# Weight parts that start 0 to 60 bytes past a multiple of 64, in a decoder trunk on one core

## The chip, the cores and the metric

The kernel runs on one core of a Trainium2 chip. The core has five engines that run side by side and meet at semaphores: TensorE (PE) multiplies, VectorE (DVE), ScalarE (ACT) and GpSimd (POOL) work element by element, and SyncE (SP) starts transfers. All but the transfers read and write the on-chip memory SBUF (128 partitions, each addressed in bytes) and the accumulators in PSUM. A matrix product on PE is a pair of instructions: LDWEIGHTS (in the profile "PEld") puts a 128x128 block, the weights, into the array, and MATMUL (in the profile "PE") streams the other operand, the moving one, through it. The metric is device time in microseconds (us) of one execution, lower is better; a kernel's time is the median of its runs.

## The reference

Two layers, each with three sub-layers around a residual stream of 512 tokens by 1024 features, in float32:

```python
h = modulate(x, norm_ffn1, sh1, sc1)
x = x + 0.5 * (1 + g1) * swiglu(h, ffn1_w1, ffn1_w3, ffn1_w2)        # 1024 -> 2816 -> 1024
h = modulate(x, norm_mix, sh2, sc2)
y = token_mix(h, ...)      # w_in; gated delta net and latent attention, 8 heads each; two branches; w_out
x = x + (1 + g2) * y
h = modulate(x, norm_ffn2, sh3, sc3)
x = x + 0.5 * (1 + g3) * swiglu(h, ffn2_w1, ffn2_w3, ffn2_w2)

def modulate(x, gain, shift, scale):
    return rms_norm(x, gain) * (1.0 + scale) + shift
def swiglu(h, w1, w3, w2):
    return (silu(h @ w1) * (h @ w3)) @ w2
```

The shifts, scales and gates come from a product of the conditioning vector with `ada_w`. Nearly all of the arithmetic is products of the 512-token activations with weight matrices that are read from main memory once.

## The kernel before

**Layout.** Features lie on the partitions, tokens along them: an activation is tiles of 128x512. A weight matrix is read in slabs of 128x1024 (eight blocks of 128x128), each 512 KB and used once.

**Two parts of each operand.** To keep float32 accuracy at one pass per product, each operand is split in a high part, rounded to the format fp32r, and a low part, the rest. A product is then three matmuls into one accumulator: high weights by high activations, high weights by low activations, low weights by high activations (`mm3`, line 130). In the profile the weight parts are called `whi` and `wlo`; the activation parts are `hhi` and `hlo`, or slices of the tiles `A`, `O`, `c3` and `L`.

**Where weight parts are made.** Three places make them: `slab` (line 116, most of the program: ACT copies `raw` to `whi`, line 124, and DVE subtracts, line 125), `parts` inside `weights` (line 604: the same for a whole slab at lines 606 and 607, where the feed-forward layers use sums of weight blocks and 256 tokens at a time), and `begin` (line 1473, the first product of layer 0). `whi` and `wlo` each have three buffers that are used in turn; a fourth kind of slab, given a `place`, lies in tiles `O` or `A` instead.

**How they are used.** `proj` (line 146) and `product` (line 621) make them the weights: the block that LDWEIGHTS loads is 128 columns, 512 bytes of each partition, of a slab. The moving operand is then an activation part of 512 or of 256 columns. In `mla_make` (line 1159) the sides change: the activation is the weights, and a `whi` or `wlo` of 384 or 512 columns is the moving operand.

**Order.** A tile framework places the instructions on the engines in an order of its own, except where the program asks to keep the written order; waits follow from which buffers an instruction reads and writes.

**Addresses.** The function `t` takes a buffer by its tag and the table `ALIGN`, line 72, gives the multiple at which buffers of a tag start; where it says nothing a buffer starts at a multiple of 32. In the built program the three `whi` start at bytes 141056, 145152 and 149248 of each partition and the three `wlo` at 153600, 157696 and 161792, all multiples of 256. Every other tile that is read as weights in blocks of 128 columns starts at a multiple of 64, except `identr` (186784, 32 past a multiple of 64), which is loaded 16 times. The two buffers `raw` start 32 past a multiple of 64, and the convolution (lines 750 to 759) has DVE read and write its tile `cv` at 4, 8 and 12 bytes past one.

Of the kernel before, what the change touches and what calls it, by code (L numbers as in the profile page):

```python
# [9 lines left out]
F32R = mybir.dt.float32r  # L10
# [5 lines left out]
P = 128  # L16
# [52 lines left out]
}  # L69


ALIGN = {"hhi": 2048, "hlo": 2048, "A": 2048, "kph": 256, "c3": 256, "L": 512, "O": 256, "whi": 256, "wlo": 256}


class Trunk:
    def __init__(self, ctx, tc, aps):
        self.tc = tc
        self.nc = tc.nc
        self.ap = aps
        self.sb = ctx.enter_context(tc.tile_pool(name="sb", bufs=1))  # L80
        self.ps = ctx.enter_context(tc.tile_pool(name="ps", bufs=1, space=bass.MemoryType.PSUM))
        self.count = 0
        self.pin = False
        self.ada_home = "L"
        self.units, self.body, self.ahead = [], None, None
        self.queue = []
        self.waiting = []
        self.quarters = {}
# [17 lines left out]
    def t(self, tag, shape, dt=F32):  # L106
        self.count += 1
        return self.sb.tile(list(shape), dt, tag=tag, name=f"{tag}_{self.count}", bufs=BUFS.get(tag, 1),
                            align_bytes=ALIGN.get(tag))

    def p(self, tag, shape=(P, SEQ)):
        self.count += 1
        return self.ps.tile(list(shape), F32, tag=tag, name=f"{tag}_{self.count}", bufs=BUFS[tag])


    def slab(self, src, n, place=None, home="raw", hold=False):

        nc = self.nc
        raw = self.t(home, [P, 1024])
        hi, lo = place or (self.t("whi", [P, 1024], F32R), self.t("wlo", [P, 1024], F32R))  # L120
        nc.sync.dma_start(raw[:, :n], src)
        for a in range(0, n, 512):
            s = slice(a, min(a + 512, n))
            both = [nc.scalar.copy(hi[:, s], raw[:, s]),  # L124
                    nc.vector.tensor_sub(lo[:, s], raw[:, s], hi[:, s].bitcast(F32))]  # L125
            for i in both if hold else ():
                self.order(i)
        return hi, lo
# [383 lines left out]
    def ffn(self, l, w, gate, finish, early, ahead=None):  # L512
# [88 lines left out]
        def weights(st):  # L601


            def parts(t):
                hi, lo = self.t("whi", [P, 1024], F32R), self.t("wlo", [P, 1024], F32R)
                nc.scalar.copy(hi, t)  # L606
                nc.vector.tensor_sub(lo, t, hi[:].bitcast(F32))  # L607
                return hi, lo

            yield parts(st["a11"])  # L610
            yield parts(st["f1"])
            f2, f4 = st["f1"], st["a12"]
            nc.vector.tensor_add(f2, f2, st["a11"])
            yield parts(f2)
            yield parts(f4)
            nc.vector.tensor_add(f4, f4, f2)
            yield parts(st["f3"])
            yield parts(f4)
            yield parts(st["a22"])
# [853 lines left out]
    def begin(self, ct, crow, vec, mod):  # L1473

        nc, ordered = self.nc, self.order
        self.pin = True

        ordered(nc.scalar.activation(self.t("sc4", [P, NT])[:, 0:1], self.one, AF.Silu))
        self.spin(2)
        wide = [self.p("sc") for _ in range(2)]  # L1480
        for (a, b), ps in zip(((0, SEQ), (SEQ, D)), wide):
            self.mm(ps, self.ones[0:1, :], crow[:, a:b], start=True, stop=True)

        sums = self.p("sm", [P, NT, P])
        for k in range(0, KT, 2):
            sq = [self.t("g", [P, SEQ]) for _ in range(2)]
            ordered(nc.scalar.activation(sq[0], self.x[:, k, :], AF.Square))
            if k == KT - 2:
                ordered(nc.vector.tensor_mul(sq[1], self.x[:, k + 1, :], self.x[:, k + 1, :]))
            else:  # L1490
                ordered(nc.scalar.activation(sq[1], self.x[:, k + 1, :], AF.Square))
            ordered(nc.vector.tensor_add(sq[0], sq[0], sq[1]))
            if k == 0:
                ss = sq[0]
                self.spin(2)
                continue
            if k == 2:
                ordered(nc.vector.tensor_add(sq[0], sq[0], ss))
            for i in range(NT):
                self.mm(sums[:, i, 0:1], sq[0][:, i * P:(i + 1) * P], self.one, start=k == 2 and i == 0,  # L1500
                        stop=k == KT - 2, skip_group_check=True)
        self.spin(1)
        ordered(nc.scalar.activation(self.cond, ct, AF.Silu))
        for i, ps in enumerate(wide):
            ordered(nc.scalar.activation(self.condb[:, i * SEQ:(i + 1) * SEQ], ps, AF.Silu))
        var, rn = (self.t("nv", [P, NT]) for _ in range(2))
        ordered(nc.vector.tensor_scalar(var, sums[:, :, 0], 1.0 / D, EPS, ALU.mult, ALU.add))
        nc.gpsimd.tensor_tensor(rn, var, self.power.to_broadcast([P, NT]), ALU.pow)
        shp = self.p("sm", [P, KT])
        self.hhi = self.t("hhi", [P, KT, SEQ], F32R)  # L1510
        self.hlo = self.t("hlo", [P, KT, SEQ], F32R)
        acts = self.hacts()
        gain = self.t("gain0", [P, KT])
        sc1 = self.t("sc1", [P, KT])
        ordered(nc.vector.tensor_scalar(sc1, vec[:, V_ADAB + KT:V_ADAB + 2 * KT], 1.0, None, ALU.add))
        n = BEGIN_SLABS
        prods, rb = [], None
        for k in range(KT):
            sc, sh = mod[:, KT + k:KT + k + 1], mod[:, k:k + 1]
            on_pe, on_pool = k in BEGIN_PE, k in BEGIN_POOL  # L1520
            self.ada_block(0, 1, k, mod)
            if not on_pe:
                self.ada_block(0, 0, k, mod)
            if k == 0:
                rp = self.p("po", [P, NT, P])
                for i in range(NT):
                    self.mm(rp[:, i, :], rn[:, i:i + 1].to_broadcast([P, P]), self.ident, start=True, stop=True)
                rb = rp[:].rearrange("p t c -> p (t c)")
            if k + 1 in BEGIN_PE:
                self.ada_block_pe(BEGIN_PE.index(k + 1), shp[:, k + 1:k + 2])  # L1530
            raw, hi = self.t("raw", [P, 1024])[:, :n * P], self.t("whi", [P, 1024], F32R)[:, :n * P]
            lo = self.t("wlo", [P, 1024], F32R)[:, :n * P]
            ordered(nc.vector.scalar_tensor_tensor(gain[:, k:k + 1], sc, sc1[:, k:k + 1],
                                                   vec[:, V_NORM + k:V_NORM + k + 1], ALU.add, ALU.mult))
            nc.sync.dma_start(raw, self.ap["w_begin"][k])
            h = self.t("g", [P, SEQ])
            ordered(nc.vector.scalar_tensor_tensor(h, self.x[:, k, :], gain[:, k:k + 1], rb, ALU.mult, ALU.mult))
            ordered(nc.vector.tensor_add(sh, shp[:, k:k + 1] if on_pe else sh, vec[:, V_ADAB + k:V_ADAB + k + 1]))
            ordered(nc.scalar.copy(hi, raw))
            xh, xl = acts[k]  # L1540
            ordered(nc.scalar.activation(xh, h, AF.Identity, bias=sh))
            ordered(nc.vector.tensor_sub(lo, raw, hi.bitcast(F32)))  # L1542
            if not on_pool:
                ordered(nc.vector.scalar_tensor_tensor(xl, h, sh, xh.bitcast(F32), ALU.add, ALU.subtract))
            for i, (a, b) in enumerate(HALVES):
                q = self.quarters.get((k // 2, i)) or self.quarter(k // 2, i, 4)
                ordered(nc.scalar.activation(q[:, k % 2, :], h[:, a:b], AF.Identity, bias=sh))
                if on_pool:
                    nc.gpsimd.tensor_sub(xl[:, a:b], q[:, k % 2, :], xh[:, a:b].bitcast(F32))  # L1549
            if k == 0:  # L1550
                prods = [self.p(tag) for tag in ("acc", "sc", "acc", "sc", "acc", "sm", "sm")]
            ws = [slice(m * P, (m + 1) * P) for m in range(n)]
            for w, p in zip(ws, prods):
                self.mm(p, hi[:, w], xh, start=k == 0, stop=False)
            for w, p in zip(ws, prods):
                self.mm(p, lo[:, w], xh, start=False, stop=False)
                self.mm(p, hi[:, w], xl, start=False, stop=k == KT - 1)
        ordered(nc.scalar.dma_start(self.ap["spill_c"], self.condb))
        self.pin = False
        return prods  # L1560
# [159 lines left out]
```

## Time and profile before

| what | value |
|---|---|
| median of 3 runs | 2707.18 us (2706.15 to 2711.35) |
| the profiled execution: its own time | 2707.17 us |
| its span, first to last instruction | 2705.4 us |
| PE busy, of the span | 2685.7 us, 99% |
| PEld busy | 2379.3 us, 88% |
| DVE busy | 1986.1 us, 73% |
| ACT busy | 1278.9 us, 47% |
| mean granted TensorE clock | 0.999 |
| matmuls, each with a weight load | 17042 |

"Busy" is the union of an engine's instructions in time. The duration of one matmul includes the time in which its results run out of the array, while the next has already begun: 389 ns for one of 512 columns, though the next starts 227 ns after it. So what a matmul costs in a stream is read from the distance between two starts, not from its duration; the same holds of weight loads. The chain of waits follows the work that ended last backwards, and lists in "pieces in order of time" how long it stayed on one engine, with the number of instructions.

### The profile page before, as it was taken

What the parts mean: (1) busy time and instruction counts of PE and PEld (TensorE: products, weight loads), DVE (VectorE), ACT (ScalarE), POOL (GpSimd) and SP (SyncE); (2) the same over time, 40 slices, a digit from 0 to 9 for tenths busy, and PEclk for the clock granted to TensorE, in tenths of its full rate; (3) what the DMA queues carried; (4) which work ended last, traced back from release to release, by engine and by line L of the source; (5) the groups of instructions that cost most, each with busy time, mean ns of one, the idle gap of its engine ahead of it and who ended that gap; (6) DMA issues with size and microseconds to landing.
All of it is one profiled execution on the core that took longest, in us unless ns stands there. A gap on an engine that the chain in (4) does not pass through costs nothing.

```text
span 2705.4 us, 44279 instructions
## 1 busy us (share of the span) xinstructions
PE 2685.7 (99%) x17042; PEld 2379.3 (88%) x17042; DVE 1986.1 (73%) x4113; ACT 1278.9 (47%) x2543; POOL 237.9 (9%) x375
## 2 busy tenths in 40 slices
PE   9999999999999999999999999999999999999999
PEld 7999997888888889998999999888888888998989
DVE  7887868776778777875677877786767687685745
ACT  4534454544457435443454444545434564453533
POOL 2100012000001011000010000120000111110000
PEclk9999999999999999999999999999999999999999
DMA  8778623212222554875528774232222225456642
GB/s 291 217 228 233 210 96 110 98 63 86 67 74 79 183 180 131 252 225 141 159 88 230 247 242 149 94 120 81 76 81 74 72 84 183 156 164 179 172 126 86
DMA packets 119108, 394.11 MB, mean 146 GB/s; under 512 B 13553, under 2 KB 16369, under 8 KB 118898
## 3 DMA queue, kind: packets, MB, share of 16 engines
q1 hardware_dynamic: 106370, 349.87, 38.8%
q0 software_dynamic: 10080, 36.70, 7.6%
q10 hardware_dynamic: 2448, 4.72, 0.5%
q8 instruction: 134, 2.20, 0.3%
q14 instruction: 76, 0.62, 0.1%
HBM read 376.03 MB, written 15.20 MB: 145 GB/s over the span
## 4 chain that ended last, share of the span: by engine, by line
PE 92%; DVE 4%; ACT 2%; DMA 1%; issue 1%; POOL 0%; SPq 0%; ACTq 0%; DVEq 0%; POOLq 0%
PE acc L96 65%; PE sc L96 17%; PE sm L96 6%; PE sm L101 2%; PE po L96 1%; ACT whi L124 1%; DMA raw<-in_w_out 0%; DVE wlo L125 0%; DVE L L283 0%; ACT g L1276 0%; DMA raw<-in_ffn_w 0%; PE po L101 0%; DVE wlo L1542 0%; DMA M<-in_x 0%; DVE mx L1271 0%
## 5 line engine op out<-in xcount | busy, mean ns | idle before, releaser
L124 ACT CAST whi<-raw 128x512 fp32r<-128x512 f32 (+2 forms) x548 | 315.7, 607 | 452.6 <-PE acc L96 231.1
L96 PE MATMUL acc<-hhi,whi 128*128 128x512 f32 (+1 forms) x1376 | 508.0, 369 | 0.0
L96 PE MATMUL acc<-hhi,wlo 128*128 128x512 f32 (+1 forms) x1376 | 489.4, 356 | 0.0
L96 PE MATMUL acc<-hlo,whi 128*128 128x512 f32 (+1 forms) x1376 | 488.8, 355 | 0.4 <-POOL hlo L1549 0.4
L125 DVE TENSOR_TENSOR wlo<-raw,whi 128x512 fp32r<-128x512 f32 (+2 forms) x548 | 374.8, 704 | 120.8 <-ACT whi L124 113.8
L96 PE MATMUL acc<-O,whi 128*128 128x512 f32 x1472 | 454.6, 390 | 0.0
L96 PE MATMUL acc<-A,whi 128*128 128x256 f32 (+1 forms) x1808 | 346.7, 291 | 1.1 <-ACT g L677 0.9
L96 PEld LDWEIGHTS acc<-O,whi 128*128 128x128 f32 x1472 | 274.9, 188 | 56.0
L96 PEld LDWEIGHTS acc<-hhi,wlo 128*128 128x128 f32 x1376 | 260.3, 189 | 38.5 <-DVE wlo L125 1.9
L96 PEld LDWEIGHTS acc<-A,whi 128*128 128x128 f32 x1808 | 286.0, 192 | 6.8 <-ACT g L677 1.3
L96 PE MATMUL acc<-O,wlo 128*128 128x512 f32 x736 | 286.8, 390 | 0.0
L96 PEld LDWEIGHTS acc<-hhi,whi 128*128 128x128 f32 x1376 | 261.1, 190 | 28.8 <-ACT whi L124 0.7
L96 PEld LDWEIGHTS acc<-hlo,whi 128*128 128x128 f32 x1376 | 261.2, 190 | 28.2 <-POOL hlo L1549 1.0
L96 PE MATMUL acc<-A,wlo 128*128 128x256 f32 (+1 forms) x904 | 262.6, 290 | 0.0
L606 ACT CAST whi<-L 128x1024 fp32r<-128x1024 f32 x140 | 147.2, 1052 | 201.7 <-issue 72.8
L607 DVE TENSOR_TENSOR wlo<-L,whi 128x1024 fp32r<-128x1024 f32 x140 | 171.2, 1223 | 35.9 <-ACT whi L606 35.1
L96 PEld LDWEIGHTS acc<-A,wlo 128*128 128x128 f32 x904 | 173.3, 192 | 2.5
L607 DVE TENSOR_TENSOR wlo<-raw,whi 128x1024 fp32r<-128x1024 f32 x105 | 128.5, 1224 | 60.8 <-ACT whi L606 59.8
L421 DVE SCALAR_TENSOR_TENSOR M<-acc,gate,M 128x512 f32<-128x512 f32 (+1 forms) x112 | 77.4, 691 | 128.7 <-PE acc L96 128.4
L606 ACT CAST whi<-raw 128x1024 fp32r<-128x1024 f32 x105 | 110.1, 1049 | 119.0 <-PE acc L96 47.2
L96 PEld LDWEIGHTS acc<-O,wlo 128*128 128x128 f32 x736 | 138.2, 188 | 28.8
L283 DVE SCALAR_TENSOR_TENSOR L<-L,kph 128x1024 f32<-128x1024 f32 x127 | 152.8, 1231 | 3.5 <-DMA L<-in_ada_w 3.5
(427 smaller groups left out, 5256.8 us busy)
## 6 DMA issues: line engine op xcount, KB each, us to landing
raw<-in_ffn_w SPq DMA_DIRECT2D x163, 512.0 KB, 4.3
L<-in_ada_w SPq DMA_DIRECT2D x127, 512.0 KB, 5.5
raw<-in_w_in SPq DMA_DIRECT2D x108, 512.0 KB, 3.3
L<-in_ffn_w SPq DMA_DIRECT2D x105, 512.0 KB, 4.4
L<-in_ffn_w POOLq DMA_DIRECT2D x70, 512.0 KB, 8.5
raw<-in_w_branch_a SPq DMA_DIRECT2D x16, 512.0 KB, 3.3
raw<-in_w_branch_b SPq DMA_DIRECT2D x16, 512.0 KB, 4.3
O<-in_ada_w SPq DMA_DIRECT2D x16, 512.0 KB, 4.5
```

Source lines behind the costliest of these rows:

```text
L96: i = self.nc.tensor.matmul(*a, **k)
L101: i = self.nc.tensor.transpose(*a, **k)
L124: both = [nc.scalar.copy(hi[:, s], raw[:, s]), nc.vector.tensor_sub(lo[:, s], raw[:, s], hi[:, s].bitcast(F32))]
L125: nc.vector.tensor_sub(lo[:, s], raw[:, s], hi[:, s].bitcast(F32))]
L283: self.order(self.nc.vector.scalar_tensor_tensor(raw, raw, 1.0, self.condb, ALU.mult, ALU.mult, accum_out=mod[:, o:o + 1]))
L421: self.nc.vector.scalar_tensor_tensor(self.x[:, m, a:b], ps[:, a:b], gate[:, m:m + 1], self.x[:, m, a:b], ALU.mult, ALU.add)
L606: nc.scalar.copy(hi, t)
L607: nc.vector.tensor_sub(lo, t, hi[:].bitcast(F32))
```

## The change

A new function `wt` takes the place of `t` where `whi` and `wlo` are made as buffers of their own. It takes a tile of 1040 columns instead of 1024 and gives back 1024 of them, from column d on, where d is counted up by a rule that goes through 0, 5, 10, 15, 4, 9, ... and so through all of 0 to 15. A column is 4 bytes, so a part starts 4d bytes, 0 to 60, past its buffer's start. `ALIGN` for these two tags becomes 64, so that distance is also the one to a multiple of 64. Slabs that are given a `place` in `O` or `A` stay where they were.

In the built program the buffers of `whi` start at 141056, 145216 and 149376 and those of `wlo` at 153536, 157696 and 161856, each 4160 bytes long; no other tile has moved. The instructions, their order on each engine and the semaphores that they wait for are the same, row for row. Of 17042 weight loads 12408 read `whi` or `wlo`: 748 of them start at a multiple of 64, and each of the 15 other distances has 750 to 815. Of the 480 matmuls that stream `whi` or `wlo`, 64 start at a multiple of 64.

```diff
-ALIGN = {"hhi": 2048, ..., "L": 512, "O": 256, "whi": 256, "wlo": 256}
+ALIGN = {"hhi": 2048, ..., "L": 512, "O": 256, "whi": 64, "wlo": 64}
...
         self.count = 0
+        self.homes = 0
...
+    def wt(self, tag):
+
+        d = (5 * self.homes + self.homes // 16) % 16
+        self.homes += 1
+        return self.t(tag, [P, 1024 + 16], F32R)[:, d:d + 1024]
...
-        hi, lo = place or (self.t("whi", [P, 1024], F32R), self.t("wlo", [P, 1024], F32R))
+        hi, lo = place or (self.wt("whi"), self.wt("wlo"))
...
             def parts(t):
-                hi, lo = self.t("whi", [P, 1024], F32R), self.t("wlo", [P, 1024], F32R)
+                hi, lo = self.wt("whi"), self.wt("wlo")
                 nc.scalar.copy(hi, t)
                 nc.vector.tensor_sub(lo, t, hi[:].bitcast(F32))
...
-            raw, hi = self.t("raw", [P, 1024])[:, :n * P], self.t("whi", [P, 1024], F32R)[:, :n * P]
-            lo = self.t("wlo", [P, 1024], F32R)[:, :n * P]
+            raw, hi = self.t("raw", [P, 1024])[:, :n * P], self.wt("whi")[:, :n * P]
+            lo = self.wt("wlo")[:, :n * P]
```

More of the change, by code (lines that the diff above doesn't have):

```diff
@@ L69 @@
 }
-ALIGN = {"hhi": 2048, "hlo": 2048, "A": 2048, "kph": 256, "c3": 256, "L": 512, "O": 256, "whi": 256, "wlo": 256}
+ALIGN = {"hhi": 2048, "hlo": 2048, "A": 2048, "kph": 256, "c3": 256, "L": 512, "O": 256, "whi": 64, "wlo": 64}
 class Trunk:
```

## The prediction, made before the changed kernel was run

> **What bounds the kernel now.** I read the page's first part, then its chain of waits, then the starts of single instructions on PE.
>
> ```profile
> PE 2685.7 (99%) x17042; PEld 2379.3 (88%) x17042; DVE 1986.1 (73%) x4113; ACT 1278.9 (47%) x2543; POOL 237.9 (9%) x375
> PE 92%; DVE 4%; ACT 2%; DMA 1%; issue 1%; POOL 0%; SPq 0%; ACTq 0%; DVEq 0%; POOLq 0%
> PEclk9999999999999999999999999999999999999999
> ```
>
> PE is never free for long, the chain that ended last lies on it for 92% of the span, and its clock is granted in full in each slice. So the question is what sets the distance between two matmul starts: the columns that are streamed, or the weight load that each one needs. The longest pieces of the chain, in order of time, give that distance (start, length, where, instructions):
>
> ```profile
> 105.28 5.76 PE acc L96 x48
> 453.87 57.14 PE acc L96 x252
> ```
>
> The first piece is all matmuls of 256 columns: 5.76 / 48 = 120 ns from start to start. The second is all of 512: 57.14 / 252 = 227 ns. The 256 columns between them cost 107 ns, so a matmul costs 107 ns for each 256 columns and 13 ns beside; at both widths the stream sets the pace. How fast weights can be loaded is seen where matmuls are short (PE's timeline: start, length, operation):
>
> ```profile
> 603.66 1.06 PE L96 MATMUL sm<-O,A 128*128 128x128 f32 x8
> 604.55 0.60 PE L101 MATMUL sm<-const,O 128*128 128x128 f32 x4
> ```
>
> Eight starts in 604.55 - 603.66 = 0.89 us are 111 ns each, though 128 columns would stream in 107 / 2 + 13 = 67 ns. So 111 ns is the load's own pace for a 128x128 block. Behind a 256-wide matmul a load has 120 - 111 = **9 ns to spare**, behind a 512-wide one 227 - 111 = **116 ns**. These two numbers carry the forecast: the change does not touch what is streamed in 12408 of its matmuls, only where their weights are read.
>
> **The change part by part.** No instruction is added, removed or moved, no wait is new, and no transfer writes into a weight part; there is only the address. Four kinds of access see it.
>
> *Loads behind a stream.* The 12408 loads divide by the width of their matmul into 6600 at 256 and 5808 at 512 columns. The groups of weight loads and matmuls are many; the largest of each kind:
>
> ```profile
> L96 PEld LDWEIGHTS acc<-O,whi 128*128 128x128 f32 x1472 | 274.9, 188 | 56.0
> L96 PEld LDWEIGHTS acc<-A,whi 128*128 128x128 f32 x1808 | 286.0, 192 | 6.8 <-ACT g L677 1.3 <-ACT g L686 0.4
> L96 PE MATMUL acc<-A,whi 128*128 128x256 f32 x1680 | 307.3, 283 | 1.1 <-ACT g L677 0.9 <-ACT g L686 0.2
> ```
>
> If memory is read in pieces of some size, a block of 512 bytes that starts inside a piece needs one piece more. In pieces of 32 bytes that is 17 for 16, 111 x 1/16 = 6.9 ns, under the 9 that are free: nothing. In pieces of 64 bytes it is 9 for 8, 111 / 8 = 13.9 ns: 4.9 too many at 256 columns, nothing at 512. The trace has one tile of full blocks that lies off a multiple of 64, `identr`, by 32 bytes, which straddles 64-byte pieces like any other distance. Here it stands behind 128-wide matmuls, where nothing hides a load, and then an aligned block in the same position:
>
> ```profile
> 445.14 1.05 PE L96 MATMUL sc<-A 128*128 128x128 f32 x8
> 445.95 0.48 PE L96 MATMUL sm<-neg,identr 128*128 128x512 f32 x1
> 446.26 0.39 PE L96 MATMUL acc<-hhi,whi 128*128 128x512 f32 x1
> ...
> 602.28 0.39 PE L96 MATMUL sc<-s,g 128*128 128x128 f32 x2
> 602.42 0.48 PE L96 MATMUL acc<-hhi,wlo 128*128 128x512 f32 x1
> 602.74 0.40 PE L96 MATMUL acc<-hhi,whi 128*128 128x512 f32 x1
> ```
>
> The matmul with `identr` takes 446.26 - 445.95 = 0.31 us to the next start, the aligned one 602.74 - 602.42 = 0.32. The tile's own view says the same:
>
> ```profile
> L96 PEld LDWEIGHTS sm<-neg,identr x16: 186/186/192, 409.9 to 1793.5; 128*128 128x128 f32 x16
> L96 PEld LDWEIGHTS acc<-hhi,whi x1376: 186/188/217, 19.8 to 2650.4; 128*128 128x128 f32 x197
> ```
>
> (least, median, most ns.) A load 32 bytes off is not longer than an aligned one, so I take **0** for this part. It is one distance of fifteen; the fourteen others no row shows with a full block. Upper bound by pieces: 6600 x 0.94 (the share off a multiple of 64) x 4.9 ns = 30 us. Lower bound: if part of the 13 ns beside the columns were a clash of a load with a stream that both begin at multiples of 64, it could shrink; 1 ns on the 11660 loads that leave such a place is -12 us, all 13 are -152 us. Of the two ends I stay at the middle, since `identr` is the nearest row and shows no difference.
>
> [...]
>
> *Loads that nothing hides.* Behind a group of short matmuls a load ends late, and the 512-wide matmul that needs it stands over 300 ns ahead of the next instead of 227. That is so 303 times; an early and the last one:
>
> ```profile
> 392.88 0.48 PE L96 MATMUL acc<-hhi,whi 128*128 128x512 f32 x1
> 393.20 0.40 PE L96 MATMUL acc<-hlo,whi 128*128 128x512 f32 x1
> ...
> 2263.80 0.49 PE L96 MATMUL acc<-O,wlo 128*128 128x512 f32 x1
> 2264.13 0.39 PE L96 MATMUL acc<-O,whi 128*128 128x512 f32 x1
> ```
>
> Here each ns counts in full: 0 by the `identr` row, 303 x 13.9 = 4 us by pieces of 64 bytes. I take 0.
>
> *Streams from a weight part.* The 480 matmuls in `mla_make`:
>
> ```profile
> L96 PE MATMUL acc<-whi,L 128*128 128x384 f32 x192 | 55.3, 342 | 0.0
> L96 PE MATMUL acc<-whi,L 128*128 128x512 f32 x128 | 47.2, 409 | 0.0
> L96 PE MATMUL acc<-wlo,L 128*128 128x384 f32 x96 | 32.5, 338 | 0.0
> L96 PE MATMUL acc<-wlo,L 128*128 128x512 f32 x64 | 26.0, 405 | 0.0
> ```
>
> The stream is the bound, so nothing hides a slower one, and 416 of the 480 leave a multiple of 64. No wide stream of the trace is off one. Below: nothing. Above, one more piece of 64 bytes in 32, about 214 / 32 = 7 ns: 416 x 7 = 3 us. I take 0, because the nearest row with a shifted operand, DVE's below, shows none.
>
> *Writing and reading the parts on ACT and DVE.*
>
> ```profile
> L753 DVE SCALAR_TENSOR_TENSOR cv<-acc,vec,cv 128x511 f32<-128x511 f32 x48 | 35.6, 742 | 0.2
> L753 DVE SCALAR_TENSOR_TENSOR cv<-acc,vec,cv 128x509 f32<-128x509 f32 x48 | 35.5, 740 | 19.4 <-ACT cv L750 19.0
> L753 DVE SCALAR_TENSOR_TENSOR cv<-acc,vec,cv 128x510 f32<-128x510 f32 x48 | 35.4, 737 | 0.1
> L421 DVE SCALAR_TENSOR_TENSOR M<-acc,gate,M 128x512 f32<-128x512 f32 x88 | 65.9, 748 | 119.7 <-PE acc L96 119.4
> ...
> L606 ACT CAST whi<-L 128x1024 fp32r<-128x1024 f32 x140 | 147.2, 1052 | 201.7 <-issue 72.8 <-PE acc L96 56.2 <-DVE L L613 25.7
> L606 ACT CAST whi<-raw 128x1024 fp32r<-128x1024 f32 x105 | 110.1, 1049 | 119.0 <-PE acc L96 47.2 <-issue 42.4 <-DVE raw L616 13.4
> ...
> L607 DVE TENSOR_TENSOR wlo<-raw,whi 128x1024 fp32r<-128x1024 f32 x105 | 128.5, 1224 | 60.8 <-ACT whi L606 59.8
> ```
>
> Line 753 reads and writes `cv` 4, 8 and 12 bytes past a multiple of 64, in 737 to 742 ns; line 421, the same operation on aligned tiles, takes 748 for 512 columns. ACT reads `raw`, 32 bytes off, in 1049 ns and the aligned `L` in 1052. That ACT writes off a multiple is the one thing without a row. So: 0. What hides a small loss is room on both engines, and it is least in the feed-forward stretches of 256 columns:
>
> ```profile
> 94.00:114.00 20.00, 20.00 (x170) 20.00 (x168) 18.54 (x24) 12.24 (x19) 1.75 (x2) 1.00 0.78 222
> ```
>
> (Busy us in 20 us: PE, PEld, DVE, ACT, POOL.) DVE has 1.46 us left there, for seven conversions: 0.2 us each.
>
> **Sum.** 0 + 0 + 0 + 0 on 2707.17, the profiled execution's own time, which is 0.01 under the median of the runs. I forecast 2707.5, with half a us for the loads that nothing hides. What stays unsure inside this case (32-byte pieces at the bare loads, 303 x 6.9 = 2 us, and 3 us of streams) spans 2702 to 2713, and that is also about what a measurement of this kernel can tell from no change, 0.2% or 5.4 us.
>
> **The rivals.**
>
> *64-byte pieces* (slower). Place: the 256-wide matmuls, whose load would need 111 + 13.9 = 125 ns against 120. Price: 30 + 4 us, so 2741. It decides as soon as a shifted load costs over 9 ns more. For it: 9 ns is little. Against it: `identr`. 6%.
>
> *Slow streams* (slower). A shifted moving operand could be fetched at half pace. Rows of 214 and 160 ns of columns (512 and 384): 192 x 214 + 288 x 160 = 87 us, of which 416 / 480 are shifted: 75 us, so 2782; if only odd columns suffer (192 of 480), 35 us and 2742. For it: the stream is the bound, with no room at all. Against it: every other engine's shifted rows. 4%.
>
> *Loads at half pace* off some multiple that 32 bytes satisfies and 4 do not. 222 ns against 120: 6600 x 0.88 x 102 = 590 us, about 3300. For it: only `identr` speaks of loads at all. Against it: a load is paced at 111 / 128 = 0.87 ns for each 4-byte element, which looks like one element at a time, and at each of the distances every element stays whole. 3%.
>
> *Slow conversions* (slower). Over 0.2 us more for each on DVE fills the feed-forward stretches; at 0.3 more, 7 x 0.3 - 1.46 = 0.64 us for each of 35 pairs of output blocks (the 140 + 105 conversions of line 606 are 35 x 7), 22 us: 2730. Against it: line 753. 4%.
>
> *A clash that goes* (faster). 12 us for each ns of the 13, at 1 ns 2695. For it: nothing in the trace varies the distance below 64 bytes, so it cannot be excluded. Against it: the distance between starts does not depend on which tile is streamed, though their addresses differ by much more than 64 bytes:
>
> ```profile
> 317.54 0.28 PE L96 MATMUL acc<-A,wlo 128*128 128x256 f32 x1
> 317.66 0.28 PE L96 MATMUL acc<-hhi,whi 128*128 128x256 f32 x1
> 317.78 0.28 PE L96 MATMUL acc<-hlo,whi 128*128 128x256 f32 x1
> ```
>
> 120 ns from `A` to `hhi` and from `hhi` to `hlo`. 5%.
>
> [...]
>
> **How the numbers follow.** 78% for the forecast, 22% for the rivals as given: 17% slower (6 + 4 + 3 + 4), 5% faster. The range takes the forecast's own span and, to hold 8 in 10, most of the way to the two nearest rivals on the slower side, where most of the rest lies: 2702 to 2740.
>
> **What would show it.** Right: in the changed profile the pieces of 48 and 252 matmuls still last 5.76 and 57.14 us, loads stay at 186 to 192 ns, lines 606 and 607 at 1.05 and 1.22 us. 64-byte pieces: 5.76 becomes about 6.0 and 57.14 stays. Half pace: 5.76 grows above 9. Slow streams: only the four groups with `whi,L` and `wlo,L` grow. Slow conversions: line 607 above 1.4 us with waits of PE on `wlo`. A clash: both pieces shrink by the same ns per matmul. Wrong altogether would be a change of the total with all these rows as before.

## The result

The changed kernel takes 2727.57 us (median, 2724.66 to 2728.39), the kernel before 2707.71 (2706.15 to 2711.35) in the runs that stand beside it: a ratio of 1.0069, interval 1.0057 to 1.0081. It is 0.7% or 19.9 us **slower**. The forecast of no change, to which I gave 78%, was wrong; the range held the time only by luck, as shown below.

**The profile after.** The page's line of busy time, its shares of the chain that ended last and its clock:

```profile
PE 2707.4 (99%) x17042; PEld 2376.4 (87%) x17042; DVE 1987.7 (73%) x4113; ACT 1278.4 (47%) x2543; POOL 237.5 (9%) x375
PE 95%; DVE 3%; ACT 2%; issue 0%; POOL 0%; DMA 0%; ACTq 0%; DVEq 0%
PEclk9999999999999999999999999999999999999999
```

Only PE's busy time has moved, 2707.4 - 2685.7 = 21.7 us, and PE is now 95% of the chain instead of 92%. The clock is granted in full as before (0.998 on the mean, 0.999 before), and no other engine has become the bound. The span is 2725.2 us against 2705.4.

What the forecast took for free did stay free, by the groups of instructions (out<-in, count | busy us, mean ns of one | idle before) and the tile's view of `identr`:

```profile
L97 PEld LDWEIGHTS acc<-O,whi 128*128 128x128 f32 x1472 | 275.0, 188 | 63.5
L97 PEld LDWEIGHTS acc<-A,whi 128*128 128x128 f32 x1808 | 282.0, 188 | 9.0 <-ACT g L684 2.9 <-ACT g L693 0.4
L97 PEld LDWEIGHTS sm<-neg,identr x16: 186/186/192, 415.0 to 1808.2; 128*128 128x128 f32 x16
L97 PE MATMUL acc<-whi,L 128*128 128x384 f32 x192 | 55.4, 343 | 0.0
L97 PE MATMUL acc<-whi,L 128*128 128x512 f32 x128 | 47.4, 411 | 0.0
L613 ACT CAST whi<-L 128x1024 fp32r<-128x1024 f32 x140 | 147.1, 1050 | 203.2 <-issue 71.8 <-PE acc L97 69.5 <-DMA L<-in_ffn_w 22.8
L614 DVE TENSOR_TENSOR wlo<-raw,whi 128x1024 fp32r<-128x1024 f32 x105 | 128.6, 1225 | 60.0 <-ACT whi L613 59.2
```

Loads of shifted weights last 188 ns (188 and 192 before), shifted streams 343 and 411 (342 and 409), the conversions 1050 and 1225 (1052 and 1224). Nothing became longer by more than 2 ns. The loss shows in the distance from one matmul to the next, in the chain's pieces in order of time (start, length, where, instructions), of the change first and then one piece of the kernel before that the prediction did not quote:

```profile
108.41 5.70 PE acc L97 x48
128.29 50.46 PE acc L97 x240
459.54 58.38 PE acc L97 x252
```

```profile
125.44 49.30 PE acc L96 x240
```

48 matmuls of 256 columns take 5.70 us, 118.8 ns each, where they took 5.76: **less**. 252 of 512 columns take 58.38 us, 231.7 ns each, where they took 57.14: **more**. The piece of 240 has both widths and grows by 1.16 us. Counted over all starts in the trace at which `whi` or `wlo` are the weights, and summed to the next start, the 512-wide matmuls take 1382.6 us (1358.9 before) and the 256-wide ones 794.1 (800.1 before). All other matmuls together, each up to the next start, add 2.1, most of it beside a few small ones; the 512-wide ones whose weights lie in `A` or `O` add only 0.1. +23.7 - 6.0 + 2.1 = 19.8 us, which is what the span grew by. So all but 2 us of the result lies in the distance between starts with `whi` and `wlo` as weights, with opposite signs at the two widths.

Within the 512-wide piece the distance is not even. These rows (PE's timeline: start, length, operation) are the first matmuls of groups of three that belong to one block of weights (high weights by high and by low activations, low weights by high ones); the two others of each group are left out:

```profile
468.25 0.39 PE L97 MATMUL acc<-hhi,whi 128*128 128x512 f32 x1
468.93 0.39 PE L97 MATMUL acc<-hhi,whi 128*128 128x512 f32 x1
469.61 0.39 PE L97 MATMUL acc<-hhi,whi 128*128 128x512 f32 x1
470.30 0.39 PE L97 MATMUL acc<-hhi,whi 128*128 128x512 f32 x1
470.99 0.40 PE L97 MATMUL acc<-hhi,whi 128*128 128x512 f32 x1
471.69 0.40 PE L97 MATMUL acc<-hhi,whi 128*128 128x512 f32 x1
```

Three matmuls take 0.68 us up to 469.61, as before the change, and 0.69 to 0.70 from there on. At that place the weights pass to another slab, and with it to another buffer and another distance: the high and low parts of the first slab start 120 and 12 bytes past a multiple of 256, those of the second 32 and 244. Nothing waits there. (That the first slab costs nothing is an exception, taken up behind the sweep.) From here on I count in such **groups of three**: before, 680 ns at 512 columns and 360 at 256.

### The profile page after: what moved, and what is told of

Read it like the earlier page. It is cut to its first block, busy times and chain, and to the rows that moved or that the text cites. A ratio compares the mean times of both kernels' runs of the same rounds, so it can differ in the third digit from the quotient of the medians.

```text
span 2725.2 us, 44279 instructions
## 1 busy us (share of the span) xinstructions
PE 2707.4 (99%) x17042; PEld 2376.4 (87%) x17042; DVE 1987.7 (73%) x4113; ACT 1278.4 (47%) x2543; POOL 237.5 (9%) x375
## 4 chain that ended last, share of the span: by engine, by line
PE 95%; DVE 3%; ACT 2%; issue 0%; POOL 0%; DMA 0%; ACTq 0%; DVEq 0%
PE acc L97 68%; PE sc L97 18%; PE sm L97 6%; PE sm L102 2%; PE po L97 1%; DVE wlo L132 0%; ACT whi L131 0%; PE po L102 0%; ACT g L1283 0%; DVE mx L1278 0%; ACT hhi L410 0%; DMA raw<-in_w_in 0%; DVE A L1243 0%; DVE s L1238 0%; POOL nv L372 0%
## 5 line engine op out<-in xcount | busy, mean ns | idle before, releaser
L97 PE MATMUL acc<-O,whi 128*128 128x512 f32 x1472 | 462.9, 396 | 0.0
L613 ACT CAST whi<-L 128x1024 fp32r<-128x1024 f32 x140 | 147.1, 1050 | 203.2 <-issue 71.8
L614 DVE TENSOR_TENSOR wlo<-L,whi 128x1024 fp32r<-128x1024 f32 x140 | 171.3, 1224 | 39.2 <-ACT whi L613 38.3
L614 DVE TENSOR_TENSOR wlo<-raw,whi 128x1024 fp32r<-128x1024 f32 x105 | 128.6, 1225 | 60.0 <-ACT whi L613 59.2
L613 ACT CAST whi<-raw 128x1024 fp32r<-128x1024 f32 x105 | 110.2, 1050 | 120.0 <-PE acc L97 48.1
```

What stands on the lines that cost most here:

```text
L97: i = self.nc.tensor.matmul(*a, **k)
```

## The experiments

The change does two things. It gives every part a distance of its own below 64 bytes, and it makes the buffers 4160 bytes long, so that they no longer lie a multiple of 256 apart: without the distances they would start 0, 64 and 128 bytes past a multiple of 256 (`whi`) and 192, 0 and 64 (`wlo`), where before all six started at a multiple of 256. Below, "place" is a weight part's start modulo 256. `hhi`, `hlo`, `A`, `O` and `L` lie at place 0 in all kernels unless it is said. The theories, in the order in which they came:

- **D**: a distance below 64 bytes costs by itself.
- **S**: the step from the high to the low part of a slab costs.
- **B**: the buffers' places modulo 256 cost.
- **L**: it is enough that all weights have the same place, whichever it is.
- **M**: what counts is the place of the weights against that of the streamed tile.
- **W**: what counts is the weights' own place, whatever is streamed.

Each edit is shown against the change unless another kernel is named. A table of all of them stands behind the last.

### Distances taken away, or made equal

**e1_zero** keeps the change's buffers and takes all distances away.

```diff
-        d = (5 * self.homes + self.homes // 16) % 16
+        d = 0
```

> Every distance is 0; the buffers of whi and wlo keep the places that the change gave them (64 bytes further from one to the next). Theory D (a load from a place off a multiple of 64 costs time by itself): as before, 2707 us, 512-wide matmuls 227 ns from start to start. Theory S (the high and the low part lie at different distances, so that loads which follow each other change their place within 64 bytes): also 2707. Theory B (the buffers are no longer 256 bytes multiples apart): as the change, 2727.

Measured: 2713.59 us, ratio 1.0022 (1.0012 to 1.0032). The chain's pieces at 256 and 512 columns:

```profile
107.07 5.64 PE acc L97 x48
456.15 58.23 PE acc L97 x252
```

117.5 and 231.1 ns each. With every part back at a multiple of 64, the buffers' places alone move both widths the way the change does: +18 us at 512, -12 at 256. That speaks for B and leaves D the rest, some 14 us.

**e2_const20** gives every part the same distance of 20 bytes, **e3_pairs_equal** gives the two parts of a slab the same one:

```diff
-        d = (5 * self.homes + self.homes // 16) % 16
+        d = 5
```

> Every part lies 20 bytes past a multiple of 64, high and low alike. Theory D: all loads are off, instead of 94% of them, so 2727 to 2729 us and 232 to 233 ns per 512-wide matmul. Theory S: no load changes its place within 64 bytes, so 2707 us and 227 ns. Theory B: 2727.

```diff
-        d = (5 * self.homes + self.homes // 16) % 16
+        n = self.homes // 2
+        d = (5 * n + n // 16) % 16
```

> The distance goes through all 16 values from slab to slab, but the high and the low part of a slab share it. Theory D: 2727 us. Theory S: only one load in 24 changes its place, so 2707 to 2709 us, with 227 ns inside a slab. Theory B: 2727.

Measured: 2727.85 (ratio 1.0077, 1.0062 to 1.0092) and 2727.06 (1.0071, 1.0056 to 1.0086), both the change's own time. That the distance varies, or differs between high and low, is worth nothing. So S falls as far as distances below 64 bytes go; the two parts of a slab still differ by a step of the buffers in both runs, and that form of S falls only with the next group of runs.

**e4_parts_only** keeps the distances only where the feed-forward layers make their parts, nearly all of them used at 256 columns.

```diff
-    def wt(self, tag):
+    def wt(self, tag, shift=False):
...
-        d = (5 * self.homes + self.homes // 16) % 16
+        d = (5 * self.homes + self.homes // 16) % 16 if shift else 0
...
-                hi, lo = self.wt("whi"), self.wt("wlo")
+                hi, lo = self.wt("whi", True), self.wt("wlo", True)
```

> Only the parts made for the 256-wide matmuls of the feed-forward layers have the distances of the change; all slabs have 0. In the change the 256-wide matmuls fell from 120 to 118.6 ns, 6 us in all, and the 512-wide rose by 24 us. If the two are independent: 2701 us, and 512-wide matmuls at 227 ns. If the fall at 256 only goes together with the rise at 512: 2707. Theory B: 2721 to 2727.

Measured: 2721.77 (1.0052, 1.0037 to 1.0067), 8.2 us above e1_zero. By starts, the 256-wide matmuls are 2.8 us and the 512-wide ones 0.8 us above it. The other 4 us stand beside four small groups of matmuls (1.5 at `sc<-O,ones`, 1.2 at `sm<-ones,g`, 1.1 at `acc<-A,O`, 0.4 at `acc<-ones`), and why is not shown. The 2701 of the expectation was missed: it took the slabs to be as in the kernel before, though their buffers lie as in e1_zero.

### One place for all weights

Next, buffers of 4352 bytes (17 x 256), so that all six have the same place. They then start at place 224 (and so does `c3`, one of the streamed tiles), and eight columns more bring a part to place 0.

**g2_all20** puts all weights at place 20, **g3_all64** at place 64.

```diff
-ALIGN = {..., "c3": 256, "L": 512, ..., "whi": 64, "wlo": 64}
+ALIGN = {..., "c3": 32, "L": 256, ..., "whi": 32, "wlo": 32}
...
-        d = (5 * self.homes + self.homes // 16) % 16
+        d = 8 + 5      # g2_all20
+        d = 8 + 16     # g3_all64
...
-        return self.t(tag, [P, 1024 + 16], F32R)[:, d:d + 1024]
+        return self.t(tag, [P, 1088], F32R)[:, d:d + 1024]
```

> The six buffers are 4352 bytes apart, so that parts at one distance all lie at the same place modulo 256; every part is 20 bytes past a multiple of 256. The run with distance 0 and buffers 64 bytes further apart left the even beat (231 and 118 ns instead of 227 and 120) and gave 2714; the ones with distances gave 2727. Theory L (the even beat needs only that all weight parts lie alike modulo 256 or less): 2707 us, 227 and 120 ns. Theory M (it needs weight parts and streamed tiles alike): 2713 us or more, 231 to 233 and 118 ns. If a distance below 64 costs by itself beside that, 2727.

> As the run before it, but every part is 64 bytes past a multiple of 256. Theory L: 2707 us, 227 and 120 ns. Theory M: 2713 us, 231 and 118 ns, as with the buffers 64 bytes further apart.

Measured: 2734.91 (1.0094, 1.0079 to 1.0109) and 2713.78 (1.0020, 1.0011 to 1.0030). The pieces of g2_all20, then of g3_all64:

```profile
108.70 5.76 PE acc L97 x48
459.57 58.80 PE acc L97 x252
```

```profile
108.51 5.44 PE acc L97 x48
231.72 5.65 PE acc L97 x48
454.47 58.80 PE acc L97 x252
```

All weights alike, and 512 columns still cost 233.3 ns: L falls, and with it the rest of S. At place 64 the 256-wide matmuls need only 113.3 ns (5.44 / 48), or 117.7 in other stretches; the groups of three take 340 or 353 ns, hardly ever anything between, and one pace lasts for up to 344 groups in a row, through changes between `hhi` and `A` as the stream. At place 20 they take about as long as at 0. So both places away from the streamed tile's are bad at 512 columns; at 256 one is good and one neutral.

These runs also answer D in its plainest form, a longer load. Behind short matmuls, where nothing hides a load, 246 of the 512-wide matmuls stand 314.9 ns ahead of the next start in the kernel before and 317.1 in the change. With all weights 20 bytes off they stand 314.2 ahead, and with all distances zero (e1_zero) 317.0. So a load from 20 bytes past a multiple of 64 is not longer.

**g5_step128** makes the buffers 4224 bytes long, without distances: the first and third buffer have place 0, the middle one 128.

```diff
-ALIGN = {..., "whi": 64, "wlo": 64}
+ALIGN = {..., "whi": 128, "wlo": 128}
...
-        d = (5 * self.homes + self.homes // 16) % 16
+        d = 0
...
-        return self.t(tag, [P, 1024 + 16], F32R)[:, d:d + 1024]
+        return self.t(tag, [P, 1056], F32R)[:, d:d + 1024]
```

> Distance 0, buffers 4224 bytes apart: four of the six at multiples of 256, the second whi and the second wlo 128 past one; the two parts of a slab lie alike. Theory L with 256: 512-wide matmuls at 227 ns but for the slab borders, 2707 to 2709. Theory M with 256: a third of the slabs leave the beat, 2709. Either with 128: 2707, 227 and 120 ns everywhere.

Measured: 2713.17 (1.0016, 1.0007 to 1.0026). Within this one kernel the slabs in the buffers of place 0 take 680 and 360 ns for a group of three (medians at 512 and 256), those at 128 take 703 and 355. So the loss follows the buffer, slab by slab, and 128 bytes are about as bad as 20 or 64 at 512 columns. The 2709 of M was too low: against the kernel before, the 512-wide matmuls lose 10.0 us and the 256-wide ones gain 4.4.

### Each width its better place

If 512 wants place 0 and 256 wants 64, give each its own. **g4_hybrid** shifts only the high parts of the feed-forward layers, **h1_parts64** both parts, with the table `ALIGN` and the buffers of 4352 bytes of g2_all20 and with `shift` as in e4_parts_only:

```diff
-        d = (5 * self.homes + self.homes // 16) % 16
+        d = 8 + (16 if shift and tag == "whi" else 0)   # g4_hybrid
+        d = 8 + (16 if shift else 0)                    # h1_parts64
```

> Buffers as in the two runs before; all parts at multiples of 256 but the high parts made for the 256-wide matmuls, which are 64 bytes past one, with their low parts at one (one of the three places that they had with distance 0 and buffers 64 bytes further apart). If each width has its beat by its own addresses: 512-wide matmuls at 227 ns as before, 256-wide at 118, 12 us less than before: 2695 us. If one kind of disturbance spreads to the other: 2707 to 2714.

> Buffers 4352 bytes apart; slabs at multiples of 256, and both parts made for the 256-wide matmuls 64 bytes past one. If what counts is the place of the weights against the streamed tiles (all at multiples of 256), separately for each width: 512-wide matmuls at 227 ns as with all parts at 0, 256-wide at 115.8 ns as with all parts at 64, which is 6600 x 4.2 ns = 24 to 28 us less than before (the 256-wide matmuls took 776.6 us in that run and 800.1 before): 2685 us. If the fall at 256 depends on what the slabs do: 2700 to 2708.

Measured: 2699.36 (0.9963, 0.9948 to 0.9977) and 2698.69 (0.9966, 0.9954 to 0.9979), both **faster** than the kernel before. Groups of h1_parts64:

```profile
L97 PE MATMUL acc<-O,whi 128*128 128x512 f32 x1472 | 455.3, 391 | 0.0
L97 PE MATMUL acc<-c,whi 128*128 128x512 f32 x128 | 40.3, 396 | 0.0
```

The 512-wide matmuls are back at 680 ns for three with `O` as the stream, and 391 ns each. With `c3` ("c" in the profile) they are not: 701 for three, 396 each, with weights at the same place 0. In these kernels `c3` itself lies at place 224, by the smaller multiple that `ALIGN` gives it. That was not intended, and it is the first sign that the streamed tile's place counts as well: for M, against W. It is also part of why g4_hybrid missed its 2695: the 256-wide matmuls gained 11.2 us, and the 512-wide ones lost 1.9.

The expected 2685 for h1_parts64 was too bold. Its 256-wide groups take 353 ns, and 340 in only 68 of 1715, where g3_all64 has 340 in 777 of 1715. At place 64 there are two paces, and these groups fall into the slower one although their weights and streams have the places that they have in g3_all64. What picks the pace is not shown; the recorded rival, that the fall at 256 hangs on what the slabs do (2700 to 2708), is not excluded.

**h2_sweep** keeps the same buffers and moves all weights through 15 places, 16 bytes apart, a place for 16 parts in turn:

```diff
-        d = (5 * self.homes + self.homes // 16) % 16
+        d = 8 + 4 * (self.homes // 16 % 15)
```

> Both parts of a slab share a distance past a multiple of 256, which goes through 0, 16, 32 ... 224 bytes, 8 slabs at each. What is wanted is the distance between matmul starts against that place. Theory M (the beat hangs on the place of the weights against the streamed tiles modulo 256): at 0 bytes 227 and 120 ns, at 64 bytes 233 and 114 to 118, at 128 bytes 232 and 119; the others are open. Theory of 32-byte places (what is a multiple of 32 costs nothing, as the one such load in the profile of before seemed to say): 227 and 120 at every multiple of 32. Time of the whole: between 2707 and 2735.

Measured: 2719.09, in one run. Median ns of a group of three, by place:

| place | 0 | 16 | 32 | 48 | 64 | 80 | 96 | 112 | 128 | 144 | 160 | 176 | 192 | 208 | 224 |
|---|---|---|---|---|---|---|---|---|---|---|---|---|---|---|---|
| 512 columns | 690 | 680 | 701 | 701 | 703 | 696 | 703 | 700 | 700 | 701 | 700 | 691 | 687 | 700 | 700 |
| 256 columns | 359 | 359 | 354 | 353 | 340 | 356 | 353 | 359 | 354 | 360 | 357 | 355 | 353 | 349 | 352 |

At 512 columns only places 0 and 16 reach 680; 32 costs 701, so a piece of 32 bytes is not the unit either. At 256 columns 64 and 208 are the best; 192 has 340 ns in 49 of its 161 groups. A place meets only eight slabs, so the medians mix it with what those slabs do anyway. At place 0 only 52 of 130 groups take 680 ns, but in the kernel before, the same 130 groups take 680 only 78 times, since most of the others stand behind short matmuls. Of those 78, 14 stream `c3`, at 224 here. Of the other 64, 50 take 680, and the 14 left follow the ones with `c3`, two after every two, with 694 and 690.

Places finer than 16 bytes bring exceptions. Among the groups that take 680 ns in the kernel before and stream a tile at place 0, the change has 50 pairs of places of a slab's two parts. Three pairs keep 680 in more than half of their groups: high part at 120 with low part at 12 (14 of 16), 144 with 100 (12 of 13), 16 with 228 (14 of 24). In e3_pairs_equal one does, 100 with 36 (31 of 41). All other pairs have medians of 687 to 733 ns in the two kernels. Each pair is met in few slabs, and no run isolates one. So the sweep gives no rule by which a place is slow.

Multiples of 16 cost about as much as g2's 20 at 512 columns: 696 to 703 ns for a group of three at eleven of the sweep's fifteen places, 700 (252 matmuls in 58.80 us) with all weights at 20.

### Moving the streamed tile instead

**i1_both64** tells M and W apart. All weights lie at place 64 as in g3_all64, and so now do the streamed `hhi` and `hlo`, while `A`, `O`, `L` and `c3` stay at 0.

```diff
-ALIGN = {"hhi": 2048, "hlo": 2048, ..., "L": 512, "O": 256, "whi": 64, "wlo": 64}
+ALIGN = {"hhi": 64, "hlo": 64, ..., "L": 256, "O": 256, "whi": 256, "wlo": 256}
...
-        d = (5 * self.homes + self.homes // 16) % 16
+        d = 16
...
-        return self.t(tag, [P, 1024 + 16], F32R)[:, d:d + 1024]
+        return self.t(tag, [P, 1088], F32R)[:, d:d + 1024]
+    def act(self, tag):
+        o = 16 if tag == "hhi" else 0
+        return self.t(tag, [P, KT * SEQ + 64], F32R)[:, o:o + KT * SEQ].rearrange("p (k s) -> p k s", k=KT)
...
-    self.hhi = self.t("hhi", [P, KT, SEQ], F32R)
-    self.hlo = self.t("hlo", [P, KT, SEQ], F32R)
+    self.hhi = self.act("hhi")
+    self.hlo = self.act("hlo")
```

> All weight parts 64 bytes past a multiple of 256, as in the run where 512-wide matmuls took 233 ns, but the streamed tiles hhi and hlo are 64 past one too; the streamed A, O, L and c3 stay at multiples of 256. Theory M (the place of the weights against the streamed tile): with hhi and hlo 227 ns at 512 and 120 at 256 come back, with A, O, L and c3 233 and 114 to 118 stay; the whole about 2707 (618 groups of three 512-wide matmuls get 20 ns back, 12 us, and 735 groups of 256-wide lose 13, 9 us, against 2714). Theory W (the place of the weights alone): 233 with every tile, 2714.

Measured: 2708.53 (0.9998, 0.9988 to 1.0007). Its timeline on PE ("x2" are two matmuls in one row), and the chain's piece of 252, which streams `hhi` and `hlo`:

```profile
112.43 0.28 PE L97 MATMUL acc<-hhi,whi 128*128 128x256 f32 x1
112.55 0.28 PE L97 MATMUL acc<-hlo,whi 128*128 128x256 f32 x1
112.67 0.28 PE L97 MATMUL acc<-hhi,wlo 128*128 128x256 f32 x1
112.79 0.28 PE L97 MATMUL acc<-hhi,whi 128*128 128x256 f32 x1
...
130.24 0.39 PE L97 MATMUL acc<-A,whi 128*128 128x256 f32 x2
130.47 0.28 PE L97 MATMUL acc<-A,wlo 128*128 128x256 f32 x1
130.58 0.39 PE L97 MATMUL acc<-A,whi 128*128 128x256 f32 x2
...
131.60 0.62 PE L97 MATMUL acc<-O,whi 128*128 128x512 f32 x2
132.06 0.39 PE L97 MATMUL acc<-O,wlo 128*128 128x512 f32 x1
132.29 0.63 PE L97 MATMUL acc<-O,whi 128*128 128x512 f32 x2
```

```profile
457.24 57.14 PE acc L97 x252
```

With weights at 64 throughout, three 256-wide matmuls take 112.79 - 112.43 = 0.36 us with `hhi` and `hlo`, at 64 too, and 130.58 - 130.24 = 0.34 with `A`, at 0. At 512 columns the 252 with `hhi` and `hlo` are back at 57.14 us to the digit, where g3_all64 needs 58.80 with the same weights, and `O` takes 132.29 - 131.60 = 0.69. Over all groups the most frequent values are 680 and 360 ns with `hhi` and `hlo` (360 in 429 of 735); with `A` at 256 columns 340 (770 of 980), and with the four other tiles medians of 698 to 700 at 512. The same weights at the same place are fast or slow by the place of what is streamed: **M is shown, for places 0 and 64, and W falls.**

**i2_parts208** is h1_parts64 with place 208, the other good one of the sweep, for the feed-forward parts, and with `c3` back at 0. Buffers of 4352 bytes at multiples of 256, `shift` as in e4_parts_only:

```diff
-ALIGN = {"hhi": 2048, "hlo": 2048, ..., "L": 512, ..., "whi": 64, "wlo": 64}
+ALIGN = {"hhi": 256, "hlo": 256, ..., "L": 256, ..., "whi": 256, "wlo": 256}
...
-        d = (5 * self.homes + self.homes // 16) % 16
+        d = 52 if shift else 0
...
-        return self.t(tag, [P, 1024 + 16], F32R)[:, d:d + 1024]
+        return self.t(tag, [P, 1088], F32R)[:, d:d + 1024]
```

> Buffers 4352 bytes apart, slabs and all streamed tiles at multiples of 256 (c3 too, which the runs with this spacing had 32 bytes before one), both parts made by the feed-forward's weights function 208 bytes past one, where the sweep showed 349 ns for three 256-wide matmuls most often and 353 at the worst. They are 5880 matmuls: 5880 x (120 - 116.4) = 21 us less than before, 2687 us; at 353, 14 us, 2694. The 512-wide at 227 ns.

Measured: 2694.54 (0.9951, 0.9934 to 0.9967), the fastest kernel here by its median (its interval overlaps that of h1_parts64): 14 us under the kernel before and 33 under the change. The start of its page (the profiled execution took 2690.6, the quickest of the four), its pieces, and the row that was slow in h1_parts64:

```profile
span 2688.8 us, 44279 instructions
...
PE 2669.4 (99%) x17042; PEld 2362.8 (88%) x17042; DVE 1984.9 (74%) x4113; ACT 1277.8 (48%) x2543; POOL 237.5 (9%) x375
```

```profile
105.46 5.60 PE acc L97 x48
125.06 49.17 PE acc L97 x240
450.64 57.14 PE acc L97 x252
```

```profile
L97 PE MATMUL acc<-c,whi 128*128 128x512 f32 x128 | 39.5, 389 | 0.0
```

The 512-wide matmuls stand exactly where they stood before the change (57.14 us, 389 ns with `c3`), and the 256-wide ones need 116.7 ns instead of 120. Of their 1715 groups of three in the feed-forward parts 1695 take 349 to 352 ns. The expected gain was 21 us; by starts the 256-wide matmuls take 784.2 us, 15.9 less than before. Against h1_parts64, from which it differs in two things, both widths are 2.9 us lower.

### All of them

The mean distances are those between two starts of one width with nothing between (some 5190 at 512 columns, 6550 at 256); the ratio is to the kernel before on the same chip.

| kernel | places of the weight parts | us | ratio | ns at 512 | ns at 256 |
|---|---|---|---|---|---|
| before | 0 | 2707.71 | 1 | 227.9 | 120.0 |
| the change | 0, 64, 128, 192, and 0 to 60 on top | 2727.57 | 1.0069 | 232.4 | 118.7 |
| e1_zero | 0, 64, 128, 192 | 2713.59 | 1.0022 | 231.3 | 117.7 |
| e2_const20 | the same + 20 | 2727.85 | 1.0077 | 232.6 | 118.5 |
| e3_pairs_equal | as the change, equal in a pair | 2727.06 | 1.0071 | 232.8 | 118.7 |
| e4_parts_only | as the change in `parts`, else e1_zero | 2721.77 | 1.0052 | 231.3 | 118.6 |
| g2_all20 | 20 | 2734.91 | 1.0094 | 233.1 | 119.8 |
| g3_all64 | 64 | 2713.78 | 1.0020 | 233.4 | 115.8 |
| g5_step128 | 0, 128, 0 | 2713.17 | 1.0016 | 229.6 | 119.3 |
| g4_hybrid | 0; high parts in `parts` 64 | 2699.36 | 0.9963 | 228.2 | 118.1 |
| h1_parts64 | 0; in `parts` 64 | 2698.69 | 0.9966 | 228.2 | 117.8 |
| h2_sweep | 0 to 224 in turn | 2719.09 | – | 231.9 | 118.2 |
| i1_both64 | 64, and `hhi`, `hlo` at 64 | 2708.53 | 0.9998 | 231.3 | 116.7 |
| i2_parts208 | 0; in `parts` 208 | 2694.54 | 0.9951 | 227.8 | 117.0 |

## Where the prediction was right and where it was wrong

**Right:** that PE's distance between starts is the bound (PE is 95% of the chain) and the clock plays no part (0.998). That the loads, the streams from weight parts and the conversions keep their durations (188 ns; 343 and 411; 1050 and 1225): all four rivals that made something longer (64-byte pieces, half pace, slow streams, slow conversions) are refuted by the rows after the change.

**Luck.** The time lies inside 2702 to 2740, but the slower end of that range was laid out for the nearest slower rivals, 64-byte pieces and slow conversions, and neither of them happened. What did happen has no term in the sum. The half us that the sum does hold, for loads that nothing hides, no run shows as a cost of the distances: 246 such matmuls stand 317.1 ns ahead of the next start in the change and 314.9 before, but 317.0 with all distances zero (e1_zero) and 314.2 with all weights at 20 (g2_all20).

**The step that failed** is "Loads behind a stream: 0". It reasoned by slack: 9 ns and 116 ns are free behind a stream, a load is not longer, so nothing moves. The load indeed isn't longer, and the slack is indeed there. What it left out is that the distance between two streams is not a property of the stream alone. It took 107 ns for each 256 columns and 13 beside as fixed, and those 13 turn out to depend on where the weights lie against the streamed tile: at 512 columns 13 becomes about 19 (233 ns, with all weights at 20 or 64), at 256 it becomes 6 to 13 (113 to 120). The larger slack, at 512, protected nothing: that width lost 23.7 us, and the width with hardly any gained 6.0. A theory of slack had the sizes, and even the signs, the wrong way round.

**The row that misled** is `identr`. A lone load behind short matmuls shows how long a load is, and it showed that rightly. It cannot show the pace of a running series of matmuls. In h2_sweep, 32 bytes from the streamed tile, which is how `identr` lies to the tile `neg` that it meets, costs 701 ns for 680 in the series.

**The rival "a clash that goes"** (5%) named the right quantity, the 13 ns, with the wrong sign for most of the kernel: it expected both pieces to shrink, and one shrank while the other grew. The argument against it was the worst of the prediction: 120 ns from `A` to `hhi` to `hlo` were to show that addresses don't matter. But these three tiles and all the weights start at multiples of 256, so in the relation that counts the three rows were one and the same case. The distance does depend on the two operands' relative place: 252 matmuls take 57.14 us in i1_both64 against 58.80 in g3_all64 with the same places of the weights.

**The sum, mended.** The buffers' steps of 64 bytes are worth +5.9 us (e1_zero: about +18 at 512 columns, -12 at 256), the distances below 64 bytes about +14 more (about +6 at each width, the rest around them). M can hold for these 14 too, since the distances move the parts off the places that do well, 0 at 512 columns and 64 and 192 at 256; no run tests that by itself. A constant distance does as much as a varying one (2727.85 us in e2_const20, 2727.57 in the change), so "another distance for each buffer in turn" is the part of the change that matters least.

**Open.** What in the chip couples the two operands is not shown. Nor is why place 64 has two paces at 256 columns and what picks one of them: what ran before seems to count, which no run isolates. Places finer than 16 bytes were tried only mixed and at 20, and why a few mixed pairs cost nothing at 512 columns is not known. Equal places were tried at 0 and 64 only. The 4 us of e4_parts_only stay without a cause.

## What to carry to other kernels

Where matmuls follow each other without a gap, read the distance from start to start, and don't conclude from unchanged durations and free slack that nothing can change. Try the same start modulo 256 bytes for the weights and the streamed tile first where streams are 512 wide, and other relative places where they are 256 wide: here 2.5% to 3% per matmul, and 14 us of the kernel's 2708 by moving the start of the feed-forward weight parts alone. Before rows are taken as evidence that something doesn't matter, ask whether that thing differs between them at all.

## What the runs showed of the hardware

- With a new load for each matmul, the distance between starts is 226.7 ns at 512 columns and 120 at 256 when weights and streamed tile have the same place modulo 256 (0 in the kernel before; 64 in i1_both64, with 120 at 256 columns in 429 of 735 groups). With another place it is mostly 229 to 235 and 113 to 120 (g3_all64, g2_all20, g5_step128, i1_both64, the sweep). Exceptions that keep 680 ns for three at 512 columns are 16 bytes in the sweep and a few mixed pairs of places in the change and in e3_pairs_equal.
- At 256 columns and place 64 the pace takes one of two values, 340 or 353 ns for a group of three, and keeps it for up to 344 groups (g3_all64). At place 20 there is no such pair: the groups spread from 349 to 368 ns (g2_all20).
- Writing a tile on ACT or DVE at mixed distances of 0 to 60 bytes cost nothing on the mean (1050 ns for 1052, 1225 for 1224), nor did loading weights from there (188 ns; where nothing hides the load, 314.2 ns to the next start at 20 bytes against 314.9 at 0).
